# Loads of the modulation weights issued on POOL's queue instead of SP's

## The chip, the cores and the metric

The kernel runs on one core of a Trainium2 chip (trn2). The metric is device microseconds (us) of one execution. Engines are named as in the profile: PE is TensorE, PEld its weight loads, DVE is VectorE, ACT is ScalarE, POOL is GpSimd, SP is SyncE, which here does nothing but issue DMAs. SPq and POOLq are the sequencers of SP and POOL.

## The reference

One layer of a decoder trunk, x of 256 rows by 2048 columns, all in float32. A conditioning row c makes six modulation rows, of 2048 values each:

```
mod = (silu(c) @ ada_w[l] + ada_b[l])             # 2048 x 12288 weights
sh1, sc1, g1, sh2, sc2, g2 = split(mod, 6)
h = modulate(rms_norm(x, norm1_g[l]), sh1, sc1)   # h * (1 + scale) + shift
proj = h @ w_in[l] + b_in[l]                      # 11264 columns
... RG-LRU branch, sliding-window attention branch, both gated and summed into merged
x = x + g1 * (merged @ w_o[l])
h2 = modulate(rms_norm(x, norm2_g[l]), sh2, sc2)
x = x + g2 * ((silu(gate) * up) @ w_ffn_out[l])   # gate, up = split(h2 @ w_ffn_in[l], 2)
return rms_norm(x, final_g)
```

## The kernel before, in words

All weights are streamed once from HBM. The layer's products are a list of 552 items; an item is a load of 512 KB (`raw`, 128 x 1024 float32; 256 KB for some of the first ones), a split of it into a high part `hi` (a cast on ACT, line 274) and a remainder `lo` (a difference on DVE, line 286), and the matmuls high x high, high x low and low x high (lines 319 to 321, and 1089 in the last product). There are five `raw` buffers, four `hi` and three `lo`, so a `raw` load waits until the `lo` of the load five before it is made.

The modulations are not made by PE: their weights are loaded transposed, a load (`aw`, 128 x 1024, 512 KB) per half row block, and DVE multiplies it by silu(c), kept as `crow`, and sums (line 406, one `CUSTOM_DVE` of some 1.28 us and a short read of the sum). Five of the six modulations, sh1, sc1, g1, sh2 and sc2, go this way (source `ada_t`, 158 loads). The sixth, g2, comes later from `ada_g` (32 loads), where DVE adds each load times c into the accumulator `pa` (line 573). One class issues both, `Halves`: its `fetch` (line 366) takes a buffer and issues the load at line 377. There are N_ADA = 2 buffers of its own (`araw`); only in the first part of the input projection may it also borrow up to N_SPARE = 5 general ones (`b4`). A small piece of sc1, the first 128 columns, is made on PE instead (loads `ak`, matmul `sc_ps`, line 151), so that the first `h` is there early.

The order of the work is the order in which the code issues it, engine by engine. A planner in the code (`step`, line 297) keeps an estimated clock of PE, DVE, ACT and DMA: ahead of every item it issues the `raw` load six items on, then `hi`, `lo`, and calls `fetch`, and it places pieces of side work (`aw` products, norms, mixers) on DVE and ACT where its clock leaves room. So `aw` and `raw` loads alternate on SP's queue in the order of the code. An engine's queue is worked in order: where its head waits for a buffer, what stands behind waits too.

At the start the order is written out: x transposed (`xT`, four loads), its squares on ACT (line 170) and sums on DVE (lines 172 and 176), the row sums on PE (`ssc`), 1/rms, the broadcast `rx`, the first `h`, and the first projection matmul (`w`, line 319). Six `aw` loads, then four more, are issued there between the first `raw` loads (`fetch_to`, line 1219). POOL makes the identity mask at the start, two triangular masks at lines 708 and 712, and clears `pa` at line 565. It issues no DMA.

Of the kernel before, what the change touches and what calls it, by code (L numbers as in the profile page):

```python
# [65 lines left out]
def hybrid_layer(  # L66
# [3 lines left out]
    nc = tc.nc  # L70
# [20 lines left out]
    def b4(name, dt=F32, shape=(4, S)):  # L91
        used["b4"] += 1
        return bp.tile([P, *shape], dt, tag="b4", name=name)
# [107 lines left out]
    def load_time(cols):  # L201

        clock["dma"] = max(clock["dma"], clock["pe"]) + cols * T_DMA
        return clock["dma"] + 2
# [154 lines left out]
    class Halves:  # L359
# [6 lines left out]
        def fetch(self):  # L366
            while self.n < min(len(self.srcs), self.limit) and clock["dma"] < clock["pe"] + self.ahead:
                if self.own < N_ADA:
                    t = wp.tile([P, CH], F32, tag="araw", name=f"aw{self.n}", bufs=N_ADA)
                    self.own += 1  # L370
                    kind = "own"
                elif self.spare():
                    t = b4(f"aw{self.n}", F32, (CH,))
                    kind = "b4"
                else:
                    return
                nc.sync.dma_start(t, self.srcs[self.n])
                self.n += 1
                self.got.append((t, kind, load_time(CH)))

# [986 lines left out]
```

## Time and profile before

| | us |
|---|---|
| median of 3 runs (1591.74 to 1596.39) | 1594.91 |
| the profiled execution | 1598.15 |
| its span | 1596.3 |
| DVE busy, share of the span | 70% |
| ACT busy, share of the span | 48% |
| mean DMA rate, 399.36 MB over the span | 250 GB/s |

The span runs from the first instruction to the last; the rest of an execution's time lies around it. Instructions that only issue a DMA are not counted as busy. A row of the view of stretches gives the stretch, its length, busy us and (x) instructions of PE, PEld, DVE, ACT and POOL, the clock that PE was granted, the share in which the 16 DMA engines were busy, and GB/s. A row of the view of waits gives who waited for whom, us in total, how often, and the longest. A row of the chain of waits gives start, length, and what it was; a DMA there counts from its issue to its landing. Matmuls overlap, and PE's ends are modelled, so PE's number of matmuls in a stretch says more than its busy time.

### The profile page before, as it was taken

How to read it: one execution, taken by the hardware profiler on the slowest of the kernel's cores; microseconds unless marked ns; L12 is line 12 of the kernel's file. 1: busy time of each engine (PE TensorE's matmuls, PEld its weight loads, DVE VectorE, ACT ScalarE, POOL GpSimd, SP SyncE). 2: the span in 40 equal slices, each digit the busy share in tenths (PEclk: the TensorE clock that was granted, in tenths of full speed). 3: DMA queues.
4: the chain of work that ended last, by engine and by line, in shares of the span. 5: the costliest groups of instructions: out<-in, count | busy, mean ns of one | idle time of the engine just before them, and what ended most of it. 6: DMA issues, size and time to landing. Idle time of an engine off the chain costs nothing.

```text
span 1596.3 us, 22536 instructions
## 1 busy us (share of the span) xinstructions
PE 1571.4 (98%) x8522; PEld 1358.2 (85%) x8522; DVE 1124.5 (70%) x1427; ACT 770.2 (48%) x973; POOL 4.8 (0%) x9
## 2 busy tenths in 40 slices
PE   8999999999999999999999999999999999999997
PEld 5999999998888887878998887888888888888886
DVE  6789988989988888788757877445545544444465
ACT  4754444485965455333446444444444444333343
POOL 0000000000000000000000000000000000000000
PEclk9999999999999999999999999999999999999999
DMA  8998998767588778989967899666666666656553
GB/s 306 332 341 311 333 338 280 269 217 240 194 277 283 247 274 274 312 294 315 338 184 222 306 334 321 185 187 188 194 186 188 194 186 229 234 195 195 190 196 119
DMA packets 113586, 399.36 MB, mean 250 GB/s; under 512 B 12611, under 2 KB 13763, under 8 KB 113093
## 3 DMA queue, kind: packets, MB, share of 16 engines
q1 hardware_dynamic: 113190, 397.41, 75.2%
q8 instruction: 66, 1.08, 0.3%
q10 hardware_dynamic: 288, 0.52, 0.1%
q14 instruction: 42, 0.34, 0.1%
HBM read 393.69 MB, written 4.19 MB: 249 GB/s over the span
## 4 chain that ended last, share of the span: by engine, by line
PE 86%; DMA 8%; DVE 4%; issue 1%; ACT 0%; SPq 0%; DVEq 0%; ACTq 0%
PE pf L1089 11%; PE wi L321 6%; PE wi L319 6%; PE wi L320 6%; PE fg L319 4%; PE fg L320 4%; PE fg L321 4%; PE fu L320 4%; PE fu L321 4%; PE fu L319 4%; PE pl L1089 3%; DMA aw<-in_ada_t_dram 3%; DMA aw<-in_ada_g_dram 3%; PE wo L320 2%; PE wo L319 2%; PE wo L321 2%
## 5 line engine op out<-in xcount | busy, mean ns | idle before, releaser
L274 ACT CAST hi<-raw 128x1024 fp32r<-128x1024 f32 (+1 forms) x552 | 565.3, 1027 | 764.4 <-PE pf L1089 109.8
L286 DVE TENSOR_TENSOR lo<-raw,hi 128x1024 fp32r<-128x1024 f32 (+1 forms) x552 | 655.1, 1192 | 349.3 <-PE pf L1089 95.7
L321 PE MATMUL wi<-h_both,lo 128*128 128x256 f32 x784 | 222.1, 283 | 1.1 <-DVE lo L286 1.1
L319 PE MATMUL wi<-h_both,hi 128*128 128x256 f32 x784 | 222.6, 284 | 0.0
L320 PE MATMUL wi<-h_both,hi 128*128 128x256 f32 x784 | 221.8, 283 | 0.0
L321 PEld LDWEIGHTS wi<-h_both,lo 128*128 128x128 f32 x784 | 150.5, 192 | 1.5 <-DVE lo L286 1.5
L319 PEld LDWEIGHTS wi<-h_both,hi 128*128 128x128 f32 x784 | 150.5, 192 | 0.2
L320 PEld LDWEIGHTS wi<-h_both,hi 128*128 128x128 f32 x784 | 150.5, 192 | 0.2
L319 PE MATMUL fg<-hi,h_both 128*128 128x512 f32 x352 | 139.1, 395 | 0.0
L320 PE MATMUL fu<-lo,h_both 128*128 128x512 f32 x352 | 137.2, 390 | 1.0 <-DVE lo L286 1.0
L320 PE MATMUL fg<-lo,h_both 128*128 128x512 f32 x352 | 137.3, 390 | 0.0
L321 PE MATMUL fg<-hi,h_both 128*128 128x512 f32 x352 | 137.2, 390 | 0.0
L321 PE MATMUL fu<-hi,h_both 128*128 128x512 f32 x352 | 137.0, 389 | 0.0
L319 PE MATMUL fu<-hi,h_both 128*128 128x512 f32 x352 | 136.9, 389 | 0.0
L406 DVE CUSTOM_DVE_ANT_0 aw<-aw,crow,modc 128x1024 f32<-128x1024 f32 x79 | 101.1, 1281 | 19.3 <-DMA aw<-in_ada_t_dram 19.0
L406 DVE CUSTOM_DVE_ANT_0 aw<-aw,crow,vec 128x1024 f32<-128x1024 f32 x79 | 100.9, 1280 | 19.4 <-DMA aw<-in_ada_t_dram 19.1
L1089 PE MATMUL pf<-hi,fh 128*128 128x512 f32 x264 | 88.5, 389 | 0.0
L1089 PE MATMUL pf<-hi,fl 128*128 128x512 f32 x264 | 88.4, 389 | 0.0
L1089 PE MATMUL pf<-lo,fh 128*128 128x512 f32 x264 | 88.4, 389 | 0.0
L320 PEld LDWEIGHTS fu<-lo,h_both 128*128 128x128 f32 x352 | 66.1, 188 | 15.5 <-DVE lo L286 1.8
L320 PEld LDWEIGHTS fg<-lo,h_both 128*128 128x128 f32 x352 | 66.1, 188 | 14.6 <-issue 0.7
L319 PEld LDWEIGHTS fg<-hi,h_both 128*128 128x128 f32 x352 | 66.1, 188 | 14.2 <-issue 0.7
(233 smaller groups left out, 2615.1 us busy)
## 6 DMA issues: line engine op xcount, KB each, us to landing
raw<-in_w_f_dram SPq DMA_DIRECT2D x176, 512.0 KB, 3.6
raw<-in_w_in_dram SPq DMA_DIRECT2D x160, 512.0 KB, 6.8
aw<-in_ada_t_dram SPq DMA_DIRECT2D x158, 512.0 KB, 6.0
raw<-in_w_f2a_dram SPq DMA_DIRECT2D x44, 512.0 KB, 4.2
raw<-in_w_lru_dram SPq DMA_DIRECT2D x32, 512.0 KB, 6.6
raw<-in_w_att_dram SPq DMA_DIRECT2D x32, 512.0 KB, 7.7
raw<-in_w_o_dram SPq DMA_DIRECT2D x32, 512.0 KB, 6.5
aw<-in_ada_g_dram SPq DMA_DIRECT2D x32, 512.0 KB, 5.7
```

The costliest lines, as they stand in the source:

```text
L274: nc.scalar.copy(hi[:, :cols], live[i][0][:, :cols])
L286: nc.vector.tensor_tensor(lo[:, :cols], raw[:, :cols], f32(hi[:, :cols]), op=ALU.subtract)
L319: nc.tensor.matmul(ps, lhsT=lh, rhs=rh, start=start, stop=False, skip_group_check=True)
L320: nc.tensor.matmul(ps, lhsT=lh, rhs=rl, start=False, stop=False, skip_group_check=True)
L321: nc.tensor.matmul(ps, lhsT=ll, rhs=rh, start=False, stop=stop, skip_group_check=True)
L406: nc.vector.tensor_tensor_reduce(out=r, in0=r, in1=crow[:, j * CH:(j + 1) * CH], op0=ALU.mult, op1=ALU.add, scale=1.0, scalar=dst if j els ...
L1089: nc.tensor.matmul(fin[t, n], lhsT=l[:, rows(t)], rhs=w[:, c0:c0 + 512], start=kt == 0 and k == 0, stop=kt == (EARLY if (t, n) == (1, 3) e ...
```

## The change

The load in `Halves.fetch` is issued on POOL's queue. Nothing else is edited.

```diff
                 else:
                     return
-                nc.sync.dma_start(t, self.srcs[self.n])
+                nc.gpsimd.dma_start(t, self.srcs[self.n])
                 self.n += 1
                 self.got.append((t, kind, load_time(CH)))
```

190 instructions move from SP to POOL; PE, DVE and ACT keep their order. At the start, on SP's queue before (`ak` the piece of sc1, `aw` modulation weights, `raw` weights of the input projection):

```order
L132 DMA ak_111<-in_ada_k_dram 128x256
L377 DMA aw_168<-in_ada_t_dram 128x1024
L377 DMA aw_170<-in_ada_t_dram 128x1024
L265 DMA raw_172<-in_w_in_dram 128x512
L265 DMA raw_174<-in_w_in_dram 128x512
L265 DMA raw_176<-in_w_in_dram 128x512
L265 DMA raw_178<-in_w_in_dram 128x512
L377 DMA aw_180<-in_ada_t_dram 128x1024
L377 DMA aw_182<-in_ada_t_dram 128x1024
```

On POOL's queue after the change, from the identity mask on, with what each waits for (DVE is VectorE, DMASW are POOL's own earlier loads):

```order
masks.py:199 AFFINE_SELECT ident<-ident 128x128 [waits Pool_49]
L377 DMA aw_168<-in_ada_t_dram 128x1024
L377 DMA aw_170<-in_ada_t_dram 128x1024
L377 DMA aw_180<-in_ada_t_dram 128x1024
L377 DMA aw_182<-in_ada_t_dram 128x1024
L377 DMA aw_184<-in_ada_t_dram 128x1024
L377 DMA aw_186<-in_ada_t_dram 128x1024
L377 DMA aw_252<-in_ada_t_dram 128x1024 [waits DVE_49]
L377 DMA aw_254<-in_ada_t_dram 128x1024 [waits DVE_49]
L377 DMA aw_256<-in_ada_t_dram 128x1024 [waits DMASW0_49]
```

The first six `aw` loads stood behind the four of x and the eight of `ak`; now they stand behind one small POOL instruction and wait for nothing.

In the middle of the program, where the attention output projection (`w_att`) begins, SP's queue before, with its waits (DMAHW are SP's own earlier loads):

```order
L377 DMA aw_6617<-in_ada_t_dram 128x1024 [waits DMAHW0_49,DVE_49]
L265 DMA raw_6619<-in_w_att_dram 128x1024 [waits DMAHW1_49,Activation_49]
L265 DMA raw_6638<-in_w_att_dram 128x1024 [waits DMAHW2_49,Activation_49]
L377 DMA aw_6644<-in_ada_t_dram 128x1024 [waits DMAHW3_49,DVE_49]
L265 DMA raw_6659<-in_w_att_dram 128x1024 [waits DMAHW4_49,Activation_49]
L377 DMA aw_6665<-in_ada_t_dram 128x1024 [waits DMAHW5_49,DVE_49]
L265 DMA raw_6679<-in_w_att_dram 128x1024 [waits DMAHW6_49,Activation_49]
```

The same place on SP's queue after the change:

```order
L265 DMA raw_6619<-in_w_att_dram 128x1024 [waits DMAHW6_49,DVE_49]
L265 DMA raw_6638<-in_w_att_dram 128x1024 [waits DMAHW7_49,DVE_49]
L265 DMA raw_6659<-in_w_att_dram 128x1024 [waits DMAHW0_49,DVE_49]
L265 DMA raw_6679<-in_w_att_dram 128x1024 [waits DMAHW1_49,DVE_49]
L265 DMA raw_6702<-in_w_att_dram 128x1024 [waits DMAHW2_49,DVE_49]
```

The `raw` loads now stand one behind the other and wait for their own buffers alone; the `aw` loads stand on POOL's queue in their old order, each still waiting for DVE. On that queue they also pass POOL's few own instructions: the two masks, between the loads 65 and 66 of `ada_t`,

```order
L377 DMA aw_2721<-in_ada_t_dram 128x1024
L377 DMA aw_2755<-in_ada_t_dram 128x1024
L708 AFFINE_SELECT mask<-mask 128x128
L712 AFFINE_SELECT mask<-mask 128x128
L377 DMA aw_2800<-in_ada_t_dram 128x1024
```

and the clearing of `pa`, behind the first load of `ada_g`. The two mask instructions were alone on POOL's queue at that place before.

## Prediction

> **What bounds the kernel now.** I read the page first, then the busy time in stretches, then the waits of the stretches in which TensorE falls short, then the chain of waits there.
>
> ```profile
> span 1596.3 us, 22536 instructions
> PE 1571.4 (98%) x8522; PEld 1358.2 (85%) x8522; DVE 1124.5 (70%) x1427; ACT 770.2 (48%) x973; POOL 4.8 (0%) x9
> PE 86%; DMA 8%; DVE 4%; issue 1%; ACT 0%; SPq 0%; DVEq 0%; ACTq 0%
> ```
>
> TensorE is busy 98% of the span, but 8% of the chain that ended last are DMAs. The next rows say where: 40 us each, the number behind PE is its matmuls, at the end stand the DMA engines' share and GB/s.
>
> ```profile
> 640.00:680.00 40.00, 39.23 (x172) 31.84 (x170) 29.44 (x41) 14.39 (x14) 0.00 (x0) 1.00 0.94 315
> 680.00:720.00 40.00, 36.87 (x165) 29.42 (x166) 33.68 (x42) 15.90 (x18) 0.00 (x0) 1.00 0.89 288
> 720.00:760.00 40.00, 38.38 (x197) 32.53 (x196) 34.38 (x43) 14.64 (x15) 0.00 (x0) 1.00 0.93 321
> 1040.00:1080.00 40.00, 40.00 (x182) 33.22 (x181) 19.07 (x18) 17.20 (x19) 0.00 (x0) 1.00 0.65 196
> ```
> ```profile
> 60.00:280.00 220.00, 220.00 (x1766) 216.91 (x1765) 195.15 (x293) 107.51 (x143) 2.32 (x2) 1.00 0.92 321
> 905.00:985.00 80.00, 78.99 (x349) 64.28 (x348) 63.58 (x57) 33.40 (x36) 0.00 (x0) 1.00 0.93 327
> ```
>
> At full pace 40 us hold 182 matmuls 512 columns wide, one per 0.22 us. From 640 to 720 there are 337 in place of 364: 27 x 0.22 = 5.9 us lost; from 720 to 760 PE idles 1.6 us more, so 7.5 us in all. From 905 to 985 it is 349 in place of 364, 3.3 us. From 60 to 280 PE is never idle although the DMA engines are at 0.92. All losses after the start that this change can reach are thus about 11 us, in the two stretches where loads of modulation weights (aw) meet loads of other weights (raw) and only two aw buffers are in use. The waits there, DVE's first, then those of SP's queue, from 640 to 800:
>
> ```profile
> DVE aw L406 <- DMA aw<-in_ada_t_dram: 23.9, 18, 2.7
> PEld wa L320 <- DVE lo L286: 8.4, 7, 2.0
> ```
> ```profile
> SPq L377 <- DVE modc L406: 91.1, 33, 4.9
> SPq L265 <- DVE lo L286: 16.6, 10, 4.0
> ```
>
> SP's queue, which issues both kinds, stands 91.1 of 160 us at an aw load (L377) until VectorE gives its buffer back, and only 16.6 us at a raw load (L265). So the raw loads queue behind the aw loads. The chain from 640 to 690:
>
> ```profile
> 643.62 7.76 DMA raw<-in_w_att_dram
> ...
> 651.62 6.33 DMA aw<-in_ada_t_dram
> ...
> 662.83 7.41 DMA aw<-in_ada_t_dram
> ...
> 674.60 7.90 DMA raw<-in_w_att_dram
> ```
>
> Two kinds of link alternate: a raw load that SP issued late, and the loop of an aw buffer (issued, landed, multiplied, given back).
>
> **The change part by part.** 190 issues leave SP's queue for POOL's; no transfer is added and no engine but SP and POOL gets another order. Four things follow.
>
> *The start.* On SP the first aw loads stood behind x and ak:
>
> ```profile
> 1.01 0.29 POOL masks.py:199 TENSOR_SCALAR_AFFINE_SELECT ident<-ident 128x128 f32<-128x128 f32 x1
> ...
> 1.82 1.86 SPq L123 DMA_DIRECT2D xT<-in_x_t_dram  x4
> 3.72 8.27 SPq L132 DMA_DIRECT2D ak<-in_ada_k_dram  x8
> ...
> 12.00 1.09 ACT L165 ACTIVATE crow<-c_ps 128x512 f32<-128x512 f32 x2
> 12.03 0.91 SPq L377 DMA_DIRECT2D aw<-in_ada_t_dram  x2
> ...
> 12.95 1.17 ACT L170 ACTIVATE sqx<-xT 128x512 f32<-128x512 f32 x2
> ...
> 21.94 0.58 PE L319 MATMUL w<-h_both,hi 128*128 128x256 f32 x1 [2.25 <-ACT h_both L448]
> ...
> 33.18 1.28 DVE L406 CUSTOM_DVE_ANT_0 aw<-aw,crow,vec 128x1024 f32<-128x1024 f32 x1 [0.88 <-DMA aw<-in_ada_t_dram]
> ```
> ```profile
> 3.24 8.40 DMA xT<-in_x_t_dram
> ```
>
> On POOL six aw loads, 3.1 MB, stand directly behind the identity mask and wait for nothing, so they can start at 1.3 us, beside x's 2.1 MB. The last x load landed at 3.24 + 8.40 = 11.64 us. If the two queues share evenly, 2.1 MB of aw pass beside 2.1 MB of x: at the 321 GB/s of the row 60 to 280 that is 6.5 us more, but two queues together may also fill holes that one left; I take 4 us. Then the squares of the last quarter, begun at 12.95 us, had 12.95 - 11.64 = 1.3 us of cover, being behind crow on ScalarE; the first matmul of the projection (21.94) moves by 4 - 1.3 = 2.7 us. The 0.88 us that VectorE waited for aw at 33.18 go. **Start: +1.8 us**, bounds -1 (no delay, wait gone) and +7.5 (all 3.1 MB ahead: 9.7 - 1.3 - 0.9).
>
> *Raw loads freed.* SP now waits only for raw buffers. Of the four long links quoted, two are raw loads; I take that third to half of the loss that is theirs, of 7.5 us, **-3 us**; bounds 0 (the aw loop alone sets the pace) and -7.5.
>
> *The aw loops.* The trace shows no DMA on POOL, so their landing is bounded by other rows. From 640 to 760, then 905 to 985, the aw rows and VectorE's; last the raw loads where no aw loads run (1040 to 1160), issues with their median us to landing:
>
> ```profile
> L377 SPq DMA_DIRECT2D aw<-in_ada_t_dram x31: 327/328/328, 640.6 to 755.6; - x31
> L406 DVE CUSTOM_DVE_ANT_0 aw<-aw,crow,modc x16: 1278/1285/1291, 639.3 to 759.1; 128x1024 f32<-128x1024 f32 x16
> DMA to landing us min/median/max: 4.2/5.9/8.1
> ```
> ```profile
> L377 SPq DMA_DIRECT2D aw<-in_ada_g_dram x22: 327/328/328, 905.7 to 983.0; - x22
> DMA to landing us min/median/max: 5.0/5.7/8.0
> ```
> ```profile
> raw<-in_w_f_dram SPq DMA_DIRECT2D x43, 512.0 KB, 3.5
> ```
>
> 31 loads in 120 us are one per 3.87 us, a loop of 7.7 us for each of the two buffers: 5.9 landing, 1.3 multiplication, the rest hand-over. The loop is the pace: each us on a landing costs 31 / 2 = 15.5 us here and, with 22 loads in 80 us (3.64 each, a loop of 7.3), 11 us there. Shorter landings give back no more than the 7.5 + 3.3 us that PE now loses. Bounds: 3.5 us, a load with the DMA engines to itself (all 11 us back), and 8.1 us, the slowest aw (2.2 x 26.5 = +58 us). I take the row that it is nearest to, the same transfers in the same traffic: POOL's smallest select takes 0.29 us where SP's issue takes 0.33, and sharing with raw loads replaces queueing behind them. **Loops: 0.**
>
> [...]
>
> *Crowding.* From 60 to 280 the DMA engines are at 0.92 and aw loads, of which N_ADA + N_SPARE = 7 may be ahead there, no longer queue behind raw loads. PE has no idle time to show; I take **+1 us**, bounds 0 and +4 (two or three 512 KB loads ahead at 321 GB/s, 1.6 us each). POOL's own waits cost nothing: the two mask selects wait once for VectorE's memset, with loads ahead already landed, and pa's memset stands behind the first ada_g load when crow is long free.
>
> Sum: 1.8 - 3 + 0 + 1 = -0.2 us, on the profiled execution's own 1598.15 us (span 1596.3 and 1.85 around it). That execution was 3.2 us above the median of the runs shown, 1594.91; on the median the sum is **1595 us**. I call under 0.3% (4.8 us) no change, about what a measurement of this kernel can tell.
>
> **The rivals.**
>
> *POOL's loads land later.* One mechanism: from the release of a buffer to the landing POOL takes longer than SP, by up to the 2.2 us bounded above, in the loops of the two stretches. It decides the sign from about 0.2 us on (0.2 x 26.5 = 5.3 us, over the 4.8 us). At a third of its bound, 0.7 us: 0.7 x 26.5 = 18.5, so 1613 us. For it: in these stretches only two buffers are in turn, so nothing hides a landing; against it: sharing may shorten a landing that today queues behind raw loads of 7.8 us.
>
> *VectorE keeps POOL from preparing them.* If a POOL load cannot be prepared while a VectorE instruction runs, each one waits for the rest of one: VectorE is busy 29.4 to 34.4 of 40 us with instructions of 1.28 us, so 0.5 us on average, up to 1.28; 0.5 x 26.5 = 13, 1608 us, at most 34. [...]
>
> *Faster.* Landings fall to about 5.2 us, since a POOL load need not stand behind raw loads in one queue: PE's loss of 7.5 + 3.3 us goes, and the start and the crowding cost 1.8 + 1: 1595 - 8 = 1587 us. For it: 91 us of SP's queue spent at L377, and raw landings of 7 to 8 us against 3.5 without aw loads. Against it: the bytes stay, 288 to 327 GB/s in those stretches.
>
> *It does nothing.* The loads wait for the same VectorE releases as before, so those already at the head of SP's queue start no earlier. 91 us of such waits speak for it; then also raw loads should not have been late, which the chain denies. 1595 us.
>
> **How the numbers follow.** Forecast (within 0.3%) 0.34; does nothing 0.05; later landings 0.24; VectorE's lock 0.10; faster 0.27. Of the forecast's share 0.06 lies over +4.8 us by the start's bound. So faster 0.27, same 0.33, slower 0.40. For 8 in 10 the range runs from 1584 (start free and all 11 us back) to 1620 (landings 1 us later, 26.5 us, less 1.5). The forecast's own range is 1590 to 1600.
>
> **What would show it.** Start: the last x load lands near 15 to 16 us, the first projection matmul near 24.6. Raw freed: ScalarE's waits for raw loads from 640 to 800 shrink, and their landing there falls below 7 us. Loops: aw loads 3.9 us apart from 640 to 760 and VectorE's waits for them near 24 us; twice that is the second case, none of it the faster one. Lock: POOL's issues end when VectorE's instructions end. Wrong altogether would be a loss between 60 and 280, where PE now has none.

## The result and the profile after

The changed kernel takes 1635.7 us (median of 4 runs, 1632.36 to 1646.36) beside 1595.65 us of the kernel before (4 runs, 1591.74 to 1596.44): ratio 1.0263, interval 1.0242 to 1.0283. That is 40 us slower, and 16 us above the top of the predicted range. The profiled execution took 1635.14 us; its span is 37.0 us longer than before's. From its page, the head, the engines' busy time and the chain that ended last:

```profile
span 1633.3 us, 22588 instructions
PE 1583.9 (97%) x8522; PEld 1361.0 (83%) x8522; DVE 1122.7 (69%) x1427; ACT 770.8 (47%) x973; POOL 105.1 (6%) x199
PE 51%; issue 35%; DMA 7%; POOL 3%; DVE 3%; ACT 0%; SPq 0%; POOLq 0%; DVEq 0%
```

No engine that counts has more to do: DVE is busy 1122.7 us (1124.5 before), ACT 770.8 (770.2), and POOL's 105.1 us are nearly all the issue of 190 loads, 0.53 us each. In the chain TensorE has fallen from 86% to 51%, and "issue", which was 1%, is 35%. That share is no measure of the loss: from about 250 to 900 us the chain runs along POOL's queue, and "issue" is there the time between two of POOL's loads, 94 us of it in one piece from 804.67 us on. So no engine works longer, and the time has to be looked for in the waits. The stretches that the prediction rested on, after the change (length, busy us and number of instructions of PE, PEld, DVE, ACT, POOL, the clock granted to PE, the DMA engines' share, GB/s):

```profile
640.00:680.00 40.00, 37.74 (x164) 30.24 (x164) 30.51 (x44) 16.55 (x16) 5.28 (x10) 1.00 0.89 299
680.00:720.00 40.00, 37.31 (x160) 29.85 (x159) 29.59 (x36) 13.61 (x14) 5.28 (x10) 0.96 0.89 295
720.00:760.00 40.00, 35.31 (x160) 28.06 (x159) 32.11 (x41) 14.67 (x16) 4.75 (x9) 1.00 0.86 284
60.00:280.00 220.00, 219.82 (x1762) 216.53 (x1761) 192.76 (x284) 111.52 (x155) 32.37 (x59) 1.00 0.94 327
920.00:960.00 40.00, 36.52 (x155) 28.91 (x154) 27.28 (x26) 14.19 (x17) 4.75 (x9) 0.96 0.85 287
960.00:1000.00 40.00, 35.99 (x156) 28.00 (x155) 28.77 (x27) 15.61 (x17) 5.28 (x10) 1.00 0.86 285
```

From 60 to 280 nothing is lost (1762 matmuls, 1766 before). In the stretches with aw loads and two buffers PE now does 155 to 164 matmuls in 40 us where full pace was 182, and the DMA engines' share, 0.89 to 0.94 before, is 0.85 to 0.89: they are not fuller, they are asked less. Taking each matmul of before and the same one of after, counted within its line and tiles, gives the shift of the program along the way (places in before's time): +8.9 us by 82 us, +1.5 more by 645, +9.0 in the stretch of the output projections of attention (called the **first loop** below, 645 to 850), +17.2 in the feed-forward with ada_g (the **second loop**, 850 to 1060), and nothing after: 36.6 us.

The waits of after, in the first loop (655 to 825 us), whole for POOL and VectorE:

```profile
POOL aw L377 <- DVE modc L406: 121.8, 34, 6.2
ACT hi L274 <- PE wa L321: 51.2, 25, 5.7
DVE aw L406 <- DMA aw<-in_ada_t_dram: 34.1, 22, 4.2
```

and in the second (880 to 1040 us), first of before, then of after:

```profile
DVE pa L573 <- DMA aw<-in_ada_g_dram: 21.2, 22, 2.4
```
```profile
DVE pa L573 <- DMA aw<-in_ada_g_dram: 40.0, 22, 4.2
```

The wait for the buffer moved from SP's queue to POOL, as it must. What counts is VectorE's wait for the load: 34.1 us where it was 23.9 in the first loop, 40.0 where it was 21.2 in the second. ScalarE's copies now wait for TensorE (51.2 us) and less for the raw loads of w_att (6.8 us where it was 37.8). The raw loads did come sooner; here are the last rows of the page, loads with their median us to landing, before and after:

```profile
aw<-in_ada_t_dram SPq DMA_DIRECT2D x158, 512.0 KB, 6.0
...
raw<-in_w_att_dram SPq DMA_DIRECT2D x32, 512.0 KB, 7.7
raw<-in_w_o_dram SPq DMA_DIRECT2D x32, 512.0 KB, 6.5
aw<-in_ada_g_dram SPq DMA_DIRECT2D x32, 512.0 KB, 5.7
```
```profile
aw<-in_ada_t_dram POOLq DMA_DIRECT2D x158, 512.0 KB, 6.6
...
raw<-in_w_att_dram SPq DMA_DIRECT2D x32, 512.0 KB, 6.4
raw<-in_w_o_dram SPq DMA_DIRECT2D x32, 512.0 KB, 4.9
aw<-in_ada_g_dram POOLq DMA_DIRECT2D x32, 512.0 KB, 6.9
```

Raw loads gained 1.3 and 1.6 us, aw loads lost 0.6 and 1.2. The kernel traded sooner raw loads for later aw loads; which of the two sets the pace, experiments 3 and 5 show.

The start is a case of its own. After's first 40 us in order of time (start, us, engine, line, operation, and in brackets the wait before it and its releaser):

```profile
1.45 3.27 POOL L377 DMA_DIRECT2D aw<-in_ada_t_dram  x6
1.84 2.31 SPq L123 DMA_DIRECT2D xT<-in_x_t_dram  x4
4.19 13.34 SPq L132 DMA_DIRECT2D ak<-in_ada_k_dram  x8
...
17.20 1.15 ACT L170 ACTIVATE sqx<-xT 128x512 f32<-128x512 f32 x2 [0.46 <-DMA xT<-in_x_t_dram]
...
20.11 2.72 PE L151 MATMUL sc_ps<-ak,cact 128*1 128x128 f32 x12 [0.17 <-DMA ak<-in_ada_k_dram]
...
32.46 0.58 PE L319 MATMUL w<-h_both,hi 128*128 128x256 f32 x1 [2.25 <-ACT h_both L448]
```

The six loads (3.1 MB) go out at 1.45 us. The last quarter of x is squared at 17.20 instead of 12.95, and ak, 128 KB a load, is worse off: TensorE waits for it until 20.11, where before it could go on at 12.10, and the first projection matmul comes at 32.46 instead of 21.94. Not all of that is the loads. The first 16 matmuls on ak and the last 16, before:

```profile
12.10 3.28 PE L151 MATMUL sc_ps<-ak,cact 128*1 128x128 f32 x16 [1.85 <-DMA ak<-in_ada_k_dram]
16.43 1.91 PE L151 MATMUL sc_ps<-ak,cact 128*1 128x128 f32 x16
```

The last 16 after the change, and then in a second profile of the changed kernel (experiment 8):

```profile
24.55 3.57 PE L151 MATMUL sc_ps<-ak,cact 128*1 128x128 f32 x16
```
```profile
23.54 1.91 PE L151 MATMUL sc_ps<-ak,cact 128*1 128x128 f32 x16
```

TensorE ran them at about half pace in the first profile of the change, 3.57 us beside 1.91. The record of the granted clock has its first full-speed stretch from 14.9 us on in before, from 37.2 in after and from 22.9 in the second profile. There TensorE's wait for ak ended only 0.5 us sooner (19.63), but the first projection matmul came at 29.06, 3.4 us sooner. So some 3 us of the first profile's start are put down to TensorE's clock, an estimate from these starts (32.46 - 29.06 - 0.5). What the two queues moved up to 16 us (packets, MB, share of the 16 engines; q1 is SP's, q0 POOL's):

```profile
q1 hardware_dynamic: 767, 2.34, 41.9%
q0 software_dynamic: 642, 2.37, 41.5%
```

Here the two queues with work got equal halves, 41.9% and 41.5% of the engines and 2.34 and 2.37 MB.

### The profile page after: what moved, and what is told of

Same layout as the page of the kernel before. It is cut to its first block, busy times and chain, and to the rows that moved or that the text cites. A ratio compares the mean times of both kernels' runs of the same rounds, so it can differ in the third digit from the quotient of the medians.

```text
span 1633.3 us, 22588 instructions
## 1 busy us (share of the span) xinstructions
PE 1583.9 (97%) x8522; PEld 1361.0 (83%) x8522; DVE 1122.7 (69%) x1427; ACT 770.8 (47%) x973; POOL 105.1 (6%) x199
## 4 chain that ended last, share of the span: by engine, by line
PE 51%; issue 35%; DMA 7%; POOL 3%; DVE 3%; ACT 0%; SPq 0%; POOLq 0%; DVEq 0%
PE pf L1089 11%; DMA aw<-in_ada_g_dram 5%; PE fu L320 4%; PE fu L321 4%; PE fu L319 4%; PE fg L320 4%; PE fg L319 4%; PE wi L320 4%; PE fg L321 4%; PE wi L321 4%; PE wi L319 4%; PE pl L1089 3%; POOL aw L377 3%; DMA ak<-in_ada_k_dram 1%; DVE pa L573 1%
## 5 line engine op out<-in xcount | busy, mean ns | idle before, releaser
L377 POOL DMA_DIRECT2D aw<-in_ada_t_dram x158 | 83.4, 529 | 703.7 <-DVE modc L406 604.1
L320 PEld LDWEIGHTS fu<-lo,h_both 128*128 128x128 f32 x352 | 66.3, 188 | 24.9 <-DVE lo L286 11.2
```

What stands on the lines that cost most here:

```text
L320: nc.tensor.matmul(ps, lhsT=lh, rhs=rl, start=False, stop=False, skip_group_check=True)
L377: nc.gpsimd.dma_start(t, self.srcs[self.n])
```

## The experiments

Two theories stood at the beginning. **Start and loops**: the start costs 9 us, and each trip round a two-buffer loop got longer. **Fixed price**: POOL's loads land later by a fixed amount, wherever they are. Later runs ask what lengthens the loop.

**1. The start.** POOL copies one column of the last x load ahead of its first aw load, so that these stand behind x again.

```diff
-    fetch_to(2)
+    nc.gpsimd.tensor_copy(sp.tile([P, 1], F32, tag="st", name="gate"), xT[3][:, 3, S - 1:S]); fetch_to(2)
```

> All 190 loads stay on POOL's queue, but a one-column copy on POOL that reads the last quarter of x stands ahead of the first, so the six free loads start only when x has landed. Theory (the two queues share the DMA engines, x and ak get half): the first projection matmul goes back from 32.5 us to 22 to 24 us, and of the 40 us that the change cost 7 to 10 go, ratio to before 1.019 to 1.021. Rival (POOL's loads are late or slow as such, and the start waits for them): first matmul stays at 31 us or later, ratio 1.025 or more.

Measured: 1631.65 us (4 runs, 1626.29 to 1638.71), ratio 1.0229 (1.0194 to 1.0264). In its trace the copy holds the loads back and the projection starts 8.4 us earlier than in after, at the upper end of what was expected:

```profile
11.23 0.18 POOL L1223 COPY gate<-xT 128x1 f32<-128x1 f32 x1 [9.92 <-DMA xT<-in_x_t_dram]
11.35 3.28 POOL L377 DMA_DIRECT2D aw<-in_ada_t_dram  x6
...
24.09 0.58 PE L319 MATMUL w<-h_both,hi 128*128 128x256 f32 x1 [2.25 <-ACT h_both L448]
```

By 82 us the shift is 0.5 us, not 8.9. So the first 3.1 MB beside x and ak are what delays the start. In this execution the rest of the program lost 27.2 us, nearly as in after (27.7), and its span is 8.8 us shorter. But it is the fastest of the four: the median gained only 4 us, the two intervals overlap, and the ratio lies between what the two theories expected.

**2. One of the two loops back on SP.** First ada_g's loads alone go back to SP, then ada_t's alone.

```diff
-        def __init__(self, srcs):
+        def __init__(self, srcs, queue=nc.gpsimd):
+            self.queue = queue
...
-                nc.gpsimd.dma_start(t, self.srcs[self.n])
+                self.queue.dma_start(t, self.srcs[self.n])
...
-        got = Halves([ada_g[kt, :, j * CH:(j + 1) * CH] for kt in range(NK) for j in range(2)])
+        got = Halves([ada_g[kt, :, j * CH:(j + 1) * CH] for kt in range(NK) for j in range(2)], nc.sync)
```

> The 32 loads of ada_g go back to SP's queue, the 158 of ada_t stay on POOL's. Theory (each stretch in which two aw buffers set the pace pays for its own loop): the 17 us lost between 900 and 990 us of the kernel before go and nothing else, ratio to before 1.014 to 1.016, matmuls 905 to 985 at the density of before. Rival (the loss there comes from raw loads that are displaced or from DMA throughput after POOL has once run, whatever the queue of ada_g): less than half of the 17 us goes, ratio 1.020 or more.

Measured: 1626.46 us (4 runs), ratio 1.0188 (1.0161 to 1.0215). The second loop's loss is gone (-2.1 us against before, +17.2 in after). The ratio is above the 1.016 expected, since this execution lost 10.0 us ahead of the loops and 14.6 in the first. With ada_t on SP and ada_g on POOL:

> The loads of ada_t on SP's queue, only the 32 of ada_g on POOL's. Theory (the parts add up): start and 645 to 805 as before, the 17 us between 900 and 990 stay, ratio 1.009 to 1.012. Rival (the loss there came from the earlier stretches, by a shifted order of transfers): under 1.006.

Measured: 1605.42 us (7 runs, 1602.42 to 1616.67), ratio 1.0077 (1.0051 to 1.0103). The start's and the first loop's loss are gone (-0.6 and -0.8 us), the second loop loses 5.9 us. Each loop's loss hangs on its own loads. The ratio is below the 1.009 to 1.012 expected: the same 32 loads of ada_g cost 17.2 us in after and 5.9 here. Whether that speaks against a fixed price these two executions can't tell, since one and the same program gave 17.2 and 7.8 us (experiment 8).

**3. A third buffer.** A trip is the time from one load into a buffer to the next load into the same buffer. If the trip round two buffers sets the pace, a third hides it, on both queues. The edit takes one general buffer (`b4`) away to make room.

```diff
-AHEAD, N_HI, N_LO, N_ADA, N_B4 = 6, 4, 3, 2, 25
+AHEAD, N_HI, N_LO, N_ADA, N_B4 = 6, 4, 3, 3, 24
```

On POOL:

> Loads on POOL as in the change, with three aw buffers of their own in place of two (and 24 general buffers in place of 25, to make room; the planner places some side work otherwise). Theory (the latency of the loop release, issue, landing, product sets the pace, not bytes): with three loads in turn a landing of 6 to 7 us is hidden, the losses of 9 and 17 us go almost wholly, and the start's 9 us stay: ratio 1.003 to 1.008. Rival (POOL's loads lower what the DMA engines move, or displace raw loads): a third buffer adds no bandwidth, ratio 1.015 or more.

On SP, the same edit on the kernel before:

> The kernel before, loads on SP, with three aw buffers and 24 general ones. Theory: the 11 us that the kernel before itself loses in the two stretches go, less some us for a general buffer fewer: ratio 0.992 to 0.998. Rival (those stretches are bound by bytes, 310 to 330 GB/s): ratio 0.998 to 1.003; if the missing general buffer costs more than both, over 1.003.

Measured: 1594.11 us on POOL (10 runs), ratio 0.9989 (0.9977 to 1.0001); 1588.3 us on SP (4 runs), ratio 0.9956 (0.9938 to 0.9974). On POOL, the stretches of the first loop and its aw loads' landing:

```profile
640.00:680.00 40.00, 40.00 (x178) 33.14 (x177) 35.41 (x49) 17.34 (x17) 6.36 (x12) 1.00 0.96 338
680.00:720.00 40.00, 40.00 (x187) 33.28 (x186) 35.41 (x45) 16.72 (x18) 6.36 (x12) 1.00 0.97 348
```
```profile
aw<-in_ada_t_dram POOLq DMA_DIRECT2D x158, 512.0 KB, 6.8
```

PE idles no more, though POOL's loads land no sooner (6.8 us, 6.6 in after). On POOL the ratio is better than the 1.003 to 1.008 expected. The loops' shift is the same on both queues, -7.6 and -2.1 us against before, and the 6 us between the two medians are near the difference of the start's 8.0 and 1.8 us. So POOL's loads cost the loops nothing once a buffer more is there: it is the trip round two buffers, not the rate.

With the first ten aw loads left on SP and the rest on POOL, three buffers have neither loss:

```diff
-                nc.gpsimd.dma_start(t, self.srcs[self.n])
+                (nc.sync if self.n < 10 and len(self.srcs) > 2 * NK else nc.gpsimd).dma_start(t, self.srcs[self.n])
```

> Three aw buffers and 24 general ones; the first ten loads of ada_t on SP's queue as before, all later ones on POOL's. Theory (the start's 8 us are the ten loads that pass x and ak, and a third buffer hides the longer loop): ratio 0.991 to 0.996, at or below three buffers on SP alone (0.9956). Rival (POOL's loads cost elsewhere too): 0.997 or more.

Measured: 1587.89 us (9 runs), ratio 0.9956 (0.9944 to 0.9967). It beats both kernels, by the buffer alone: it is as fast as SP with three buffers, not faster.

**4. The price by itself.** A kernel that computes nothing of the layer: 24 loads like aw into two buffers, each used by one VectorE instruction, from SP alone (sa), from POOL alone (pb), then the same beside 32 raw loads from SP each (sc, pd).

```diff
+    stage(nc.sync, "sa", False)
+    stage(nc.gpsimd, "pb", False)
+    stage(nc.sync, "sc", True)
+    stage(nc.gpsimd, "pd", True)
```

> The loop by itself; nothing of the layer is computed, the output is a sum of loads. Four stages of 24 loads of ada_t in two buffers, each multiplied into a sum on VectorE: sa on SP's queue alone, pb on POOL's alone, then sc on SP's with 32 raw loads between them on the same queue, pd on POOL's with 32 raw loads on SP's (ScalarE frees a raw buffer every 2.6 us). Theory (a fixed price of POOL, 0.26 us of hand-over and 0.20 us of issue as the traces of before and after show, and sharing on top): issue to landing pb - sa 0.2 to 0.5 us, pd - sc 0.2 to 1.2 us. Rival (all of it is fixed): pb - sa as large as pd - sc, 0.7 us or more. Rival (all of it is sharing): pb - sa under 0.1 us.

Its loads with the median us to landing:

```profile
sa<-in_ada_t_dram SPq DMA_DIRECT2D x24, 512.0 KB, 4.7
pb<-in_ada_t_dram POOLq DMA_DIRECT2D x24, 512.0 KB, 4.0
sc<-in_ada_t_dram SPq DMA_DIRECT2D x24, 512.0 KB, 6.2
pd<-in_ada_t_dram POOLq DMA_DIRECT2D x24, 512.0 KB, 6.2
```

The issue takes POOL 0.53 us (SP 0.33), and from the release of the buffer to the issue, the hand-over, it is 0.30 us (SP 0.03), yet alone the load lands 0.7 us sooner, counted from the start of its issue, and beside raw loads as soon. Both expectations were wrong, and the theory of a landing that is later by a fixed amount falls. The trips are another matter. The loads beside raw loads, with their first and last start:

```profile
L84 SPq DMA_DIRECT2D sc<-in_ada_t_dram x24: 327/328/328, 138.6 to 223.9; - x24
L84 POOL DMA_DIRECT2D pd<-in_ada_t_dram x24: 527/527/530, 228.9 to 320.1; - x24
```

24 loads are 23 steps, 11.5 trips: in this one execution 7.42 us on SP and 7.93 on POOL, 0.5 us more, about what hand-over and issue add (0.27 and 0.20). Alone the trips are equal (24 loads start within 66.3 and 65.9 us).

**5. How dear the trip is.** POOL clears half of the buffer ahead of each ada_g load, which delays the issue.

```diff
+                if len(self.srcs) == 2 * NK: nc.gpsimd.memset(t[:, :512], 0.0)
                 nc.gpsimd.dma_start(t, self.srcs[self.n])
```

> The change, and for the 32 loads of ada_g alone POOL clears half of the buffer ahead of each load, so the loop is longer by the memset, 0.4 to 0.6 us, and its hand-over. Theory (the loop is the pace there): each us on the loop costs 16 us, so 8 to 12 us on top of the change, ratio to before 1.031 to 1.034. Rival (the pace is set by raw loads or bytes): under 3 us, ratio 1.027 or less.

Measured: 1643.4 us (4 runs), ratio 1.0314 (1.0288 to 1.034), 7.7 us above the change. Release to issue in that loop went from 0.30 to 0.88 us; 0.58 us on 30 loads in two buffers are 0.58 x 15 = 8.7 us. So what is added to a trip is paid, about in full by the medians, though the two intervals leave much room. The profiles alone would not have shown it: this one lost 18.9 us in the second loop, the two of the change 17.2 and 7.8 (see the last experiment).

**6. Which half of the change lengthens the trip.** The change does two things at once: POOL issues, and raw loads no longer stand behind aw loads. Two kernels have one of them each. In the first the raw loads go to POOL and aw stays on SP; in the second both go to POOL, in the old order; the first eight raw and ten aw loads stay on SP, so the start is as before. In a third only that start is restored.

```diff
-        nc.sync.dma_start(raw[:, :cols], src)
+        (nc.sync if i < 8 else nc.gpsimd).dma_start(raw[:, :cols], src)
```

> The two kinds of load change places: the modulations' loads stay on SP's queue as before, and the other weights' raw loads, all but the first eight, are issued by POOL. The start is as before, so the whole difference is that of the loops. Theory 'lost place' (the modulations' transfers slow down because the raw loads no longer stand behind them in one queue, whichever engine issues): the loops lose here too, 8 to 17 us, ratio 1.005 to 1.011, with the modulations' landings at 640 to 805 and in the second loop at 6.2 us or more. Theory 'POOL's hand-over' (the loop is longer by what POOL adds to each of its own loads, 0.26 us from release to issue and 0.20 us of issue): the modulations' loads are prompt on SP, nothing is lost, ratio 0.998 to 1.002, landings as before (mean 6.1 and 5.7 us) or shorter. Both together: about 1.003 to 1.005.

> All loads of weights after the first eight raw ones and the first ten of the modulations go to POOL's queue, in the one order that SP had before: the raw loads stand behind the modulations' again, but POOL issues. Theory 'lost place': only the hand-over is left, 0.26 us and perhaps 0.20 us of issue over about 60 loads in two buffers, 7 to 12 us by my sensitivity of 26 us for one us, ratio 1.004 to 1.008, and less than the kernel that has the modulations alone on POOL. Theory 'POOL's hand-over': the same loss as the kernel with the modulations alone on POOL or more, since each load also waits behind the 0.53 us of issue of the raw loads ahead of it: 1.012 to 1.020.

> The changed kernel with the first ten loads of the modulations left on SP, in their old place, so that only the loops are changed. Both theories: the start's 9 us are gone and the loops' loss stays: 12 to 27 us, ratio 1.008 to 1.017 (the kernel that only held POOL's first loads back until the input was there had 1.019 to 1.026; if this one is at 1.02 or more, the loops alone cost nearly all and the start's 9 us do not reach the end). The first projection's first matmul at 22 us from the span's start, as before.

Measured: raw on POOL 1606.84 us (6 runs), ratio 1.0072 (1.0053 to 1.0092); all on POOL 1603.09 us (5 runs), ratio 1.0059 (1.0037 to 1.0081); only the start restored 1635.7 us (4 runs), ratio 1.0249 (1.0223 to 1.0275). The same 33 loads of the first loop and 30 of the second, in each kernel (issue ns min/median/max, first and last start). Before, then after:

```profile
L377 SPq DMA_DIRECT2D aw<-in_ada_t_dram x33: 327/328/328, 646.9 to 771.6; - x33
...
L377 SPq DMA_DIRECT2D aw<-in_ada_g_dram x30: 327/328/328, 879.2 to 983.0; - x30
```
```profile
L377 POOL DMA_DIRECT2D aw<-in_ada_t_dram x33: 527/527/530, 661.9 to 791.4; - x33
...
L377 POOL DMA_DIRECT2D aw<-in_ada_g_dram x30: 527/527/530, 898.8 to 1018.6; - x30
```

Raw on POOL, then all on POOL, then only the start restored:

```profile
L377 SPq DMA_DIRECT2D aw<-in_ada_t_dram x33: 327/328/328, 646.3 to 773.8; - x33
...
L377 SPq DMA_DIRECT2D aw<-in_ada_g_dram x30: 327/328/333, 880.7 to 990.2; - x30
```
```profile
L377 POOL DMA_DIRECT2D aw<-in_ada_t_dram x33: 527/527/530, 649.0 to 776.9; - x33
...
L377 POOL DMA_DIRECT2D aw<-in_ada_g_dram x30: 527/527/537, 884.6 to 988.1; - x30
```
```profile
L377 POOL DMA_DIRECT2D aw<-in_ada_t_dram x33: 527/527/530, 663.2 to 801.1; - x33
...
L377 POOL DMA_DIRECT2D aw<-in_ada_g_dram x30: 527/527/530, 907.7 to 1025.6; - x30
```

33 loads are 32 steps, 16 trips, and 30 loads 14.5 trips. Before needs 124.7 and 103.8 us, so 7.79 and 7.16 us a trip. POOL alone, with the order kept, adds 0.20 us and nothing (127.9 and 103.5 us); a queue of its own alone adds 0.18 and 0.39 us (127.5 and 109.5 us). These trips come from one execution each, and two profiles of the changed kernel differ by 0.5 and 0.6 us a trip (experiment 8: 8.58 and 7.64 us), so they don't prove the parts. The medians do: 11.9 us for the queue apart and 8.1 us for POOL's issue in the old order, both clear of noise. With raw on POOL the loss is not that of late raw loads: ScalarE waits 24.6 us for those of w_att, 37.8 before, while the aw loads' median landing in the first loop is 6.6 us, 5.9 before. With all on POOL it may be in part, since that wait is 50.5 us.

Together the two parts make 20 us in the medians. Both at once, with only the start restored, cost 40.7 us, and 0.83 and 0.97 us a trip (137.9 and 117.9 us; in after 0.30 and 1.10): more than the parts. And the start's 9 us, which this kernel does not lose, are not missed in its median.

**7. What the parts leave.** In the kernel with only the start restored, the stretches tell of something that before had not (its 645 to 680 and 720 to 760 us):

```profile
645.00:680.00 35.00, 30.10 (x121) 23.73 (x120) 24.07 (x34) 12.22 (x12) 4.23 (x8) 0.90 0.79 258
720.00:760.00 40.00, 34.48 (x142) 27.16 (x141) 27.97 (x36) 13.26 (x14) 4.75 (x9) 0.91 0.81 270
```

The clock is granted at 0.90 and 0.91, where before's stretches from 640 to 760 us had 1.00. The record of the granted clock says how: stretches of 3.41 us at half clock, each beginning in the second half of an idle time of TensorE of about 1.8 us or more or within 2 us of its end (in after at 696.0, 938.4 and 1013.4 us, behind idle times of 2.10, 2.41 and 2.17 us), and each worth up to 1.7 us of matmuls by half of 3.41 us, an estimate. In the two loops there are none in before, none with three buffers, 1 with all on POOL, 2 with raw on POOL, 3 in after and 6 here. Of the 13.2 us by which the first loop's 33 loads take longer here, 5 such stretches could make 8.5.

One theory for the rest was a head start: SP issues a raw load at once, POOL an aw load 0.46 us later, so that raw always goes first. Two or four transfers of four bytes ahead of every raw load take that away.

```diff
-        raw = wp.tile([P, CH], F32, tag="raw", name=f"raw{i}", bufs=AHEAD - 1)
-        nc.sync.dma_start(raw[:, :cols], src)
+        raw = wp.tile([P, CH + 2], F32, tag="raw", name=f"raw{i}", bufs=AHEAD - 1)
+        [nc.sync.dma_start(raw[0:1, CH + j:CH + j + 1], src[0:1, j:j + 1]) for j in range(2 * (i >= 8))]; nc.sync.dma_start(raw[:, :cols], src)
```

> The kernel with the first ten loads of the modulations on SP and the rest on POOL (it lost 2.5%), in which SP issues two transfers of four bytes ahead of every raw load after the first eight, into two columns that are added to the raw buffer and never read. If one issue takes SP 0.33 us, a raw load starts 0.66 us later than it did, which takes back the 0.46 us by which SP is quicker than POOL (0.26 of hand-over, 0.20 of issue). Theory 'head start' (of two loads whose buffers come free at about the same time, the one that starts first gets the DMA engines, and POOL is always second): most of the loss goes, to the 0.7% of the exchanged queues, ratio 1.006 to 1.012, landings of the modulations below 6.1 and 5.9 us. Theory 'sharing' (two queues share evenly whoever starts): 1.020 to 1.027, as without them. Theory 'dear issue' (the loss is what POOL adds to its loads): also 1.020 to 1.027.

> The same with four such transfers, 1.3 us by the same working. Theory 'head start': no more than the 0.6% of the loads that all go through POOL in the old order, ratio 1.003 to 1.009, unless raw loads become late themselves (then the wait of ScalarE's copies for raw shows it, in the first projections and in the feed-forward above all). Theory 'sharing' or 'dear issue': 1.020 to 1.030.

Measured: with two 1625.93 us (4 runs, 1617.75 to 1626.24), ratio 1.0173 (1.0138 to 1.0208); with four 1677.86 us (4 runs), ratio 1.0525 (1.049 to 1.0561). Two gained 10 us, less than the head start called for and, by the median, more than the others did; the interval reaches into theirs. Its two loops:

```profile
L377 POOL DMA_DIRECT2D aw<-in_ada_t_dram x33: 527/527/530, 660.1 to 790.3; - x33
...
L377 POOL DMA_DIRECT2D aw<-in_ada_g_dram x30: 527/527/530, 896.9 to 1011.1; - x30
```

They take 130.2 and 114.2 us, 7.7 and 3.7 less than without the small transfers; this execution has one stretch at half clock, not six, and 5 x 1.7 = 8.5 us is most of what its span of 1624.5 us gained on 1637.3. That the head start itself costs anything isn't shown. Four say nothing on it, since now raw loads are late in the input projection; ScalarE's wait for them from 40 to 320 us is 142.4 us, against 39.5 without the small transfers.

**8. The change once more**, for a second profile.

> The changed kernel once more, for a second profiled execution: how far the loss of the two loops differs between executions of one kernel. Median 1630 to 1640, ratio 1.022 to 1.028; between the first projection's start and 645 us the same +10 us as in the first profile if the start alone decides there, and in each loop 9 to 20 us.

Measured: 1635.37 us (4 runs, 1632.87 to 1637.77), ratio 1.0249 (1.0229 to 1.0269). The shift against before, by the same matmuls, in all kernels with aw on POOL, raw on SP and two buffers (us; the last column counts the stretches at half clock after 640 us):

```
kernel                     to 82   to 645   first loop   second loop   all    half clock
changed                     8.9      1.5        9.0         17.2       36.6       3
changed, second profile     5.3      5.6       16.9          7.8       35.6       3
first loads behind x        0.5      4.5       10.6         12.1       27.7       2
only the start restored     0.8      7.2       21.2         11.4       40.6       6
ada_g on SP                 5.9     10.0       14.6         -2.1       28.4       3
small transfers, two        0.6      7.2       10.6          9.3       27.8       1
```

The same program loses 9.0 or 16.9 us in the first loop, and 17.2 or 7.8 in the second. The expected 9 to 20 us for each loop missed by a little, and the start is no constant either, in part by TensorE's clock, as estimated above. Sums agree much better than their parts.

## Why the prediction was wrong

**The loops, 0 us: the step that failed.** The prediction took for POOL's landing "the row that it is nearest to, the same transfers in the same traffic". It wasn't the same traffic: one queue had kept each raw load behind the aw load issued before it, and the change took that order away. In the profile the two loops lost 9.0 + 17.2 = 26.2 us, in the second one 24.7. Nor was it the same issue: from the release of a buffer to the end of the issue POOL takes 0.83 us and SP 0.36. The runs split the cause in part. A queue apart costs 8.3 us in the profile and 11.9 in the medians (with the raw loads on POOL); POOL's hand-over and issue cost 4.7 and 8.1 us (with the order kept, where raw loads are later too). Both at once cost 40.7 us in the medians with the start restored, twice the sum of the two. Some of the rest is TensorE's half clock, which came after waits of about 1.8 us or more: by the estimate above up to 1.7 us a stretch, so up to 5 of the 26 us in the profile of the change and up to 10 with the start restored. What else the two add together stays open. The step's own bounds, -11 and +58, held it, its pace per us of landing too: 0.58 us more cost 7.7 us.

**The start, +1.8 us.** Sized wrong: +8.9 us in the first profile, +5.3 in the second, against a bound of 7.5; some 3 us of the first are, by the estimate above, TensorE's slower clock, which was in no term. The even sharing was right (41.9% and 41.5%), and the last squares came 17.20 - 12.95 = 4.3 us later. What the sum also had left out is ak, which stands behind x in SP's half: TensorE waited for ak to 20.11 us, longer than for x, and ScalarE's 1.3 us of cover were no cover for that. In the medians the start weighs less: with it restored they are 0 and 4 us lower, and why the loops take the rest back stays open.

**Raw loads freed, -3 us.** ScalarE's waits for raw loads shrank as foreseen and w_att's landing fell below 7 us (7.7 to 6.4; w_o's from 6.5 to 4.9), but no time was seen to come of it: the lower end, "the aw loop alone sets the pace", was the case.

**Crowding, +1 us.** 0 from 82 to 280 us in after. In other executions of kernels with this split 4 to 10 us go between 82 and 645 us, nearly all of it after 200 us, and 1.8 to 5.1 us of it before 280, where the prediction had named a loss as its sign of being wrong altogether; what decides it was not tried.

**The rivals.** "POOL's loads land later" had the place, the mechanism and a good part of the price: 0.7 us a trip for 18.5 us, where 0.3 to 1.1 us were measured; the runs show that it is not the landing after the issue, which by itself is as soon as SP's, but the 0.47 us up to the end of the issue and the lost order. VectorE's lock, a supposition of the prediction, shows no sign: POOL's issue takes 527 to 530 ns and comes 0.29 to 0.30 us after the release throughout the first loop, in which VectorE is busy 29 to 32 of 40 us. "Faster" fell with its cause, since no median aw landing in the loops got shorter where raw loads ran on a queue apart. "It does nothing" missed that the order in the queue was itself worth something.

**The range.** It ended where the loops alone cost 26.5 us less the raw loads' gain; with the start's upper bound added it would have ended at 1595 + 26.5 + 7.5 = 1629, still short: the half clock was in no bound, and of the loops' own bound of +58 us the range took less than half.

## What to carry to other kernels

A queue is also an order: where two kinds of load share one, the one that a small loop waits for may owe its landing to the others standing behind it, and a wait at the head of the queue that looks like an obstacle can be that protection: here the aw loads landed in a median of 6.0 and 5.7 us in one order with the raw loads on SP, 5.9 and 5.3 in that order on POOL, 6.6 and 6.9 after the change, on a queue apart. Before moving a load to another queue, see how many buffers its loop has; with one more buffer the same move cost nothing in the loops (-7.6 and -2.1 us against before on both queues), and with the first ten loads left on SP the buffer was worth 0.4% on either queue. At a program's start, look at what a second queue's loads will stand beside: here they took half of the rate from x and ak, 41.5% of the engines beside 41.9%.

## What the runs showed of the hardware that was not expected

TensorE's clock fell to half for 3.41 us after waits much shorter than that. In the loops of these kernels idle times from 1.79 to 2.48 us were followed by such a stretch, while others up to 2.49 us were not; of those over 3 us none went without. What separated the two is the sum within one step of a grid: in each trace all half-clock stretches begin on one grid of 3.413 us (in after at 50.89, 696.01, 938.35 and 1013.45 us, 189, 71 and 22 steps apart). In the 15 traces of the whole layer, from 60 to 1570 us, each of the 27 that began at full clock followed a step in which TensorE's matmuls, whose ends are modelled, left 1.79 us or more idle; of 6577 steps that no such stretch followed, one had more than that (1.81), the rest 1.77 at most. In after the three such steps had 2.10, 2.18 and 2.17 us, the others 1.55 at most; in before none had more than 1.16, and no stretch followed. The wait of 2.49 us lay across two steps. So waits that added up to about 1.8 us of such a step were followed by a stretch that costs up to 1.7 us more, an estimate by half of 3.41 us.

POOL's loads were not slow: 0.53 us of issue against 0.33, 0.30 us from release to issue against 0.03, and all the same 4.0 us from the start of the issue to landing against 4.7 with nothing else running. In one order with the raw loads, all on POOL, the aw loads' median landing was 5.9 and 5.3 us where SP had 6.0 and 5.7.
